# A layer of two linear-recurrence mixers: the block products of the triangular inverses run over four 32x32 tiles in slots of eight systems, and the planner's tables are set anew

## The chip, the cores and the metric

The kernel runs on one core of a Trainium2 chip. The metric is the device time of one execution in microseconds (us). The kernel before took 1860.27 us as the median of 3 runs (1856.26 to 1860.48).

## The reference, cut to what matters

One layer of a diffusion backbone works on 1024 latent tokens and 128 context tokens of width 1024, in fp32. A combined projection feeds two token mixers, an output projection follows, and then a gated MLP with a depthwise convolution. The first mixer (HGRN2) has 4 heads of 128. The second (RWKV-7) has 8 heads of 64 and this recurrence, run forwards and backwards:

```python
def step(S, inp):
    r_t, w_t, k_t, v_t, kk_t, a_t = inp
    sk = jnp.einsum('bhij,bhj->bhi', S, kk_t)
    S = (S * w_t[:, :, None, :] - sk[..., None] * (kk_t * a_t)[:, :, None, :]
         + v_t[..., None] * k_t[:, :, None, :])
    return S, jnp.einsum('bhij,bhj->bhi', S, r_t)
```

Each state update depends on the one before it through `sk`. The kernel works in chunks of 64 tokens: inside a chunk the dependence is a unit triangular 64x64 system, one for each chunk, head and direction, and the kernel forms the inverse of every one of them ahead of the recurrence.

## The kernel before, in words

**Stages.** The numbers are those of the profiled execution. From 0 to about 50 us the inputs are loaded, normalised and turned. From 50 to 500 us the combined projection runs: dense products of the normalised tokens `hh`, `hl` with weights `wh`, `wl`, each product in three parts (L1108, L1109, L1110), 128x128 weights against 384 columns. Among them lie the features of the RWKV mixer for four pairs of heads (`features`, L1346 to L1475) and, after each pair, `elim`, which makes the inverses. From 495 us the two chains of the recurrence run (`prep`, first line on TensorE L1759, then `chains`, L1803 to L1831), 18 chunk steps for each of two groups, with the HGRN blocks (L1629 to L1674), the rest of the projection and the loads of the modulation weights (`ada_block`, L1009 to L1023) among them. The output projection (L1995 to L1997) follows from about 950 us, the MLP's first half (L2104) from 1088 us and its down projection (L2253 to L2255) from 1570 us.

**The inverses.** A 64x64 triangular system is cut into 32x32 quarters. VectorE inverts the two diagonal quarters of all systems at once, one row after another (L1488, L1491, 31 steps), and turns the result with two transposes into `ttd` and `tn` (L1493, L1494). The off-diagonal quarter of the inverse is a product of three 32x32 matrices: first the middle product of `ako` with `tn` (L1507), then that result with `ttd` (L1516). Systems lie in pairs: `c2` is 0 or 1, and pair member `c2` has its upper half on partitions `64*c2` to `64*c2+31` and its lower half on the next 32. So both products of a system go from one group of 32 partitions to its neighbour. `elim` is called five times: for four pairs of heads with 32 pairs of systems each (`nu` = 32), and for the context chunks with 16.

In the kernel before, the products go in halves of 16 pairs of systems. For each half a batch of 32 products runs L1507 (two tiles of the array, one for each `c2`, each with a PSUM bank of its own), two evictions copy 32 partitions x 512 elements to `pm` (L1510), a batch of 32 products runs L1516, and two evictions copy to the result `tt` (L1519). An fp32 product counts as two MATMUL instructions in the trace, so a batch has 64. There are 9 batches of each kind. The corner of `tt` that must be zero is written by GpSimd ahead of all this (L1500), and the result goes to DRAM in 24 transfers for each call (L1530 to L1545), some of them of those zeros. The chains load it again, step by step.

**What sets the order.** Nothing is issued where it is written. A planner (`Plan`) records every operation, and a list scheduler puts each engine's operations in an order by their longest path to the end plus a lead in us: `LEADS` has one for each function, `NUDGE` one for each stretch of 64 operations. PSUM tiles come from named sets of places; the `el` set of `elim` lies on banks 6 and 7, which the chains' set `a` uses as well, and a tile of `a` isn't placed before all earlier tiles of `el` are. So the chains' first product stands behind the last batch of the context's `elim`. The order that results is fixed when the kernel is built; each engine then runs its list in order. Transfers are issued by SP or by GpSimd, whichever the planner picks.

The diff touches `elim`, `pbank`, the `el` set, `ada_block` and the two tables.

Of the kernel before, what the change touches and what calls it, by code (L numbers as in the profile page):

```python
# [34 lines left out]
EARLY = ()  # L35
LEAD_EARLY = -1.6
# [9 lines left out]
NUDGE = {1: -6, 3: 10, 38: 17, 47: 42, 56: -15, 59: 1, 63: 5, 79: -4, 90: -3, 93: 10, 94: 10, 95: -10, 96: -10, 97: 10, 98: 30, 99: 10, 100: 20, 101: -10, 108: -10, 109: -10, 110: -6, 111: -10, 114: -3, 122: -2, 129: 11, 130: 10, 131: 10, 132: 10, 134: -44, 136: 10, 138: 40, 141: -8}  # L46
LEADS = {'hgrn_block': -3.6, 'hgrn_out': 106.6, 'ada_block': 46.6, 'prep': 119.5, 'mod_scale': 90, 'const': 103.8, 'params': -71.6, 'param_loads': -28.9, 'wo_tile': 8.1, 'ffn_down': 14.5, 'chains': 18.7, 'hgrn_in': 0.0, 'features': 0.0, 'elim': -12.5, 'post': 12.6, 'conv_rkv': 0.0, 'bonus_rows': 5.2, 'turned': 2.4, 'step_kernel': -1.0}
# [753 lines left out]
def step_kernel(ctx: ExitStack, tc: tile.TileContext, I, O):  # L801
# [73 lines left out]
    at = {t: plan.tags[t].places[0][1] for t in ("tsys", "etmp", "ttd", "tn")}  # L875
    plan.tag("adaw3", [(top, at[t] + 512 * b) for t in ("ttd", "tn", "tsys") for b in range(2)], 512)
    plan.tag("adab3", [(top, at["etmp"])], 128)
    plan.tag("adam3", [(top, at["etmp"] + 128)], 128)
# [59 lines left out]
    banks("el", 6, 2)  # L938
# [9 lines left out]
    def pbank(tag="pj"):  # L948
        return tl(tag, [P, 512])
# [51 lines left out]
    def ada_block(b):  # L1001

        c0, early = 2048 + 512 * b, b in EARLY
        br = tl("adab3" if early else "adab", [4, P])
        ld(br, I["ada_b"][0, c0:c0 + 512].rearrange("(a b) -> a b", b=P))
        ps, mr = pbank("el" if early else "a"), tl("adam3" if early else "adam", [P, P])
# [3 lines left out]
        for kt in range(KT):  # L1010
            w = tl("adaw3" if early else "adaw2", [P, 512])
            ld(w, I["ada_w"][0, kt * P:(kt + 1) * P, c0:c0 + 512])
            with plan.together():
                for q in range(4):
                    mm(ps[32 * q:32 * q + 32, 0:P], sT[:, kt, :], w[:, P * q:P * q + P], False, kt == KT - 1)
# [6 lines left out]
        pq = pbank("el" if early else "a")  # L1022
# [455 lines left out]
    def elim(akd, ako, nu, name, tag):  # L1478
# [18 lines left out]
        pm = tl("asys", [P, 32, 32])  # L1497
        copy(tt[:, :, 0:32], ttd[:, :, 0:nu].rearrange("p t u -> p u t"))
        for c2 in range(2):
            pool.memset(tt[64 * c2 + 32:64 * c2 + 64, :, 32:64], 0.0)  # L1500
        for u0 in range(0, nu, 16):
            ps = [pbank(tag) for c2 in range(2)]
            with plan.together():
                for u in range(u0, u0 + 16):
                    for c2 in range(2):
                        a, b = slice(64 * c2, 64 * c2 + 32), slice(64 * c2 + 32, 64 * c2 + 64)
                        mm(ps[c2][b, (u - u0) * 32:(u - u0) * 32 + 32], ako[a, u, :], tn[a, :, u], True, True)  # L1507
            for c2 in range(2):
                b = slice(64 * c2 + 32, 64 * c2 + 64)
                copy(flat(pm[b, u0:u0 + 16, :]), ps[c2][b, :])  # L1510
            ps = [pbank(tag) for c2 in range(2)]
            with plan.together():
                for u in range(u0, u0 + 16):
                    for c2 in range(2):
                        a, b = slice(64 * c2, 64 * c2 + 32), slice(64 * c2 + 32, 64 * c2 + 64)
                        mm(ps[c2][a, (u - u0) * 32:(u - u0) * 32 + 32], pm[b, u, :], ttd[b, :, u], True, True)  # L1516
            for c2 in range(2):
                a = slice(64 * c2, 64 * c2 + 32)
                copy(tt[a, u0:u0 + 16, 32:64], ps[c2][a, :].rearrange("p (u t) -> p u t", t=32))  # L1519
# [829 lines left out]
```

## Time and profile before

| | us |
|---|---|
| median of 3 runs | 1860.27 |
| profiled execution, its own time | 1852.33 |
| its span | 1850.2 |
| TensorE busy | 1785.8 |
| VectorE busy | 1417.0 |
| ScalarE busy | 868.0 |
| GpSimd busy | 296.2 |

The profiled execution lies 7.9 us under the median of the runs. TensorE's busy time is a union of overlapping matmuls. A row of a timeline gives the start, the duration and the count of merged instructions; the time between the starts of two neighbouring rows is what the first of them costs the engine. A row of a grouped view gives the total busy time and the mean duration of one, then the idle time of the engine ahead of the group and what ended it. "issue" is time in which the engine waited for nothing that the profile shows.

### The profile page before, as it was taken

How to read it: one execution, taken by the hardware profiler on the slowest of the kernel's cores; microseconds unless marked ns; L12 is line 12 of the kernel's file. 1: busy time of each engine (PE TensorE's matmuls, PEld its weight loads, DVE VectorE, ACT ScalarE, POOL GpSimd, SP SyncE). 2: the span in 40 equal slices, each digit the busy share in tenths (PEclk: the TensorE clock that was granted, in tenths of full speed). 3: DMA queues.
4: the chain of work that ended last, by engine and by line, in shares of the span. 5: the costliest groups of instructions: out<-in, count | busy, mean ns of one | idle time of the engine just before them, and what ended most of it. 6: DMA issues, size and time to landing. Idle time of an engine off the chain costs nothing.

```text
span 1850.2 us, 45135 instructions
## 1 busy us (share of the span) xinstructions
PE 1785.8 (97%) x18369; PEld 1598.8 (86%) x18369; DVE 1417.0 (77%) x2660; ACT 868.0 (47%) x1755; POOL 296.2 (16%) x567
## 2 busy tenths in 40 slices
PE   7999999899989999999999989999999999999998
PEld 4889898799977888888778789999999999888886
DVE  7559888977778887885787688999999954896443
ACT  7556755642256544553545754444444433422321
POOL 2113425253212212212210100000000000000000
PEclk9999999999999999999999999999999999999999
DMA  9325637476667757889977611222222245775351
GB/s 324 105 74 141 153 92 189 114 206 185 198 189 223 233 177 219 268 239 288 288 247 252 211 49 59 96 72 72 72 72 72 80 144 207 244 251 191 120 172 59
DMA packets 268728, 307.44 MB, mean 166 GB/s; under 512 B 63292, under 2 KB 212842, under 8 KB 268521
## 3 DMA queue, kind: packets, MB, share of 16 engines
q1 hardware_dynamic: 241112, 220.92, 40.1%
q0 software_dynamic: 27408, 83.64, 13.3%
q8 instruction: 144, 2.36, 0.5%
q14 instruction: 64, 0.52, 0.1%
HBM read 200.50 MB, written 103.99 MB: 165 GB/s over the span
## 4 chain that ended last, share of the span: by engine, by line
PE 81%; DVE 7%; DMA 6%; issue 3%; ACT 2%; POOL 1%; SPq 0%; DVEq 0%; POOLq 0%; ACTq 0%
PE banks L2104 26%; PE banks L1108 6%; PE banks L1110 5%; PE banks L1109 5%; PE banks L2253 5%; PE banks L2254 5%; PE banks L2255 5%; PE banks L1995 2%; PE banks L1759 2%; PE banks L1996 1%; PE banks L1997 1%; DMA top<-in_ada_w_dram 1%; PE banks L1803 1%; PE banks L1810 1%; PE banks L1674 1%
## 5 line engine op out<-in xcount | busy, mean ns | idle before, releaser
L1108 PE MATMUL banks<-hh,wh 128*128 128x384 f32 x768 | 280.7, 365 | 0.0
L1110 PE MATMUL banks<-hh,wl 128*128 128x384 f32 x768 | 259.6, 338 | 0.1
L1109 PE MATMUL banks<-hl,wh 128*128 128x384 f32 x768 | 259.4, 338 | 0.0
L2193 DVE SCALAR_TENSOR_TENSOR low<-low,pf 128x1024 f32<-128x1024 f32 x176 | 224.4, 1278 | 3.5 <-ACT low L2187 2.1
L2104 PE MATMUL banks<-qm,wh 128*128 128x320 f32 x968 | 224.5, 311 | 0.0
L2104 PE MATMUL banks<-qm,wl 128*128 128x320 f32 x528 | 163.8, 310 | 3.3 <-DVE wl L2074 3.3
L2104 PE MATMUL banks<-hbm,wh 128*128 128x256 f32 x880 | 162.8, 282 | 2.4 <-DVE low L1975 1.6
L1108 PEld LDWEIGHTS banks<-hh,wh 128*128 128x128 f32 x768 | 145.9, 190 | 20.4 <-issue 12.3
L2104 PEld LDWEIGHTS banks<-qm,wh 128*128 128x128 f32 x968 | 161.9, 190 | 0.1
L1109 PEld LDWEIGHTS banks<-hl,wh 128*128 128x128 f32 x768 | 146.2, 190 | 2.0 <-issue 1.0
L1110 PEld LDWEIGHTS banks<-hh,wl 128*128 128x128 f32 x768 | 145.6, 190 | 0.0
L2104 PEld LDWEIGHTS banks<-hbm,wh 128*128 128x128 f32 x880 | 139.2, 190 | 2.8 <-ACT hbm L2037 1.8
L2104 PE MATMUL banks<-ham,wh 128*128 128x256 f32 (+1 forms) x616 | 132.4, 295 | 0.0
L2104 PE MATMUL banks<-hbm,wl 128*128 128x256 f32 x440 | 124.4, 283 | 0.0
L2104 PEld LDWEIGHTS banks<-qm,wl 128*128 128x128 f32 x528 | 99.6, 189 | 3.9 <-DVE wl L2074 3.9
L2104 PEld LDWEIGHTS banks<-ham,wh 128*128 128x128 f32 x616 | 102.4, 191 | 0.0
L2142 ACT COPY fx<-banks 128x320 f32<-128x320 f32 (+1 forms) x132 | 52.2, 396 | 84.0 <-PE banks L2104 83.8
L2074 ACT CAST wh<-fx 128x512 fp32r<-128x512 f32 x88 | 54.3, 620 | 75.1 <-PE banks L2104 65.3
L2253 PE MATMUL banks<-qm,hbm 128*128 128x512 f32 x216 | 85.6, 396 | 0.0
L2254 PE MATMUL banks<-qm,hbm 128*128 128x512 f32 x216 | 85.5, 396 | 0.0
L2255 PE MATMUL banks<-qm,hbm 128*128 128x512 f32 x216 | 85.4, 395 | 0.0
L2104 PEld LDWEIGHTS banks<-hbm,wl 128*128 128x128 f32 x440 | 83.8, 191 | 0.0
(508 smaller groups left out, 4364.4 us busy)
## 6 DMA issues: line engine op xcount, KB each, us to landing
wr<-in_w_in_dram SPq DMA_DIRECT2D x34, 512.0 KB, 6.0
top<-in_ada_w_dram SPq DMA_DIRECT2D x64, 256.0 KB, 5.5
d_a<-low POOLq DMA_DIRECT2D x22, 576.0 KB, 4.0
low<-d_ak SPq DMA_DIRECT2D x64, 192.0 KB, 4.9
low<-in_ffn_w_up_dram SPq DMA_DIRECT2D x22, 512.0 KB, 3.9
wr<-in_ffn_w_gate_dram SPq DMA_DIRECT2D x22, 512.0 KB
low<-d_kb SPq DMA_DIRECT2D x36, 256.0 KB, 3.6
low<-d_a SPq DMA_DIRECT2D x12, 704.0 KB, 4.8
```

What stands on the lines that cost most here:

```text
L1108: mm(o, wh[:, kt, :], hh[:, kt, c], kt == 0, False)
L1109: mm(o, wh[:, kt, :], hl[:, kt, c], False, False)
L1110: mm(o, wl[:, kt, :], hh[:, kt, c], False, kt == KT - 1)
L1759: mm(pa[h][:, P * w:P * w + P], kb[hc[h], w, :], W[hc[h], A0[h] + 192 * w:A0[h] + 192 * w + P], True, True)
L1995: mm(ps, oh[:, kt, :], woh, kt == 0, False)
L2074: split(*w, src)
L2104: pe.matmul(o, a[:, kt, :], b[:, kt, :], start=start and first, stop=last, skip_group_check=not start)
L2142: act.copy(keep[n], y[:, 0:w])
L2193: dve.scalar_tensor_tensor(av, shifted(dy, dx), tap(3 * dy + dx), av, MUL, ADD)
L2253: mm(o, lh, w[:, 0, c], first, False)
L2254: mm(o, lh, w[:, 1, c], False, False)
L2255: mm(o, ll, w[:, 0, c], False, last)
```

## The change

The two products of the inverses are interleaved. The systems go in groups of eight pairs, one group for each slot. Slot `k` holds the first product of group `k` (from the even groups of 32 partitions to the odd ones) and the second product of group `k-1` (from the odd to the even ones). All four groups of partitions are in use, and the four tiles take turns, product by product. All four write one PSUM tile of 256 columns, half a bank. One eviction of 128 partitions x 256 elements then moves both results to `tt`: the finished quarter to its place, and the middle product into the corner of `tt` that the next slot reads as weights. The first slot holds only first products, the last only second ones; their evictions take 32 partitions x 256 twice. A call with 32 pairs has five slots, the one with 16 has three. Since the zero corner now serves as a buffer, GpSimd writes its zeros after the last slot.

The tables that set the order are changed in a few entries, for example the lead of `elim` from -12.5 to -4.6. Code for an early block of modulation weights, which an empty list had switched off, is removed.

```diff
-NUDGE = {..., 98: 30, 99: 10, 100: 20, ..., 129: 11, 130: 10, ...}
-LEADS = {..., 'param_loads': -28.9, 'wo_tile': 8.1, ..., 'elim': -12.5, ..., 'bonus_rows': 5.2, ...}
+NUDGE = {..., 98: 47, 99: 5, 100: 20, ..., 126: 17, 127: 24, 130: 10, ...}
+LEADS = {..., 'param_loads': 9.6, 'wo_tile': 5.1, ..., 'elim': -4.6, ..., 'bonus_rows': 6.6, ...}
...
-    banks("el", 6, 2)
+    plan.tag("el", [(mp, 512 * 6 + 256 * b) for b in range(4)], 256)
...
-    def pbank(tag="pj"):
-        return tl(tag, [P, 512])
+    def pbank(tag="pj", n=512):
+        return tl(tag, [P, n])
...
-        pm = tl("asys", [P, 32, 32])
+        pm = tl("asys", [P, 8, 32])
         copy(tt[:, :, 0:32], ttd[:, :, 0:nu].rearrange("p t u -> p u t"))
-        for c2 in range(2):
-            pool.memset(tt[64 * c2 + 32:64 * c2 + 64, :, 32:64], 0.0)
-        for u0 in range(0, nu, 16):
-            ps = [pbank(tag) for c2 in range(2)]
-            with plan.together():
-                for u in range(u0, u0 + 16):
-                    for c2 in range(2):
-                        a, b = slice(64 * c2, 64 * c2 + 32), slice(64 * c2 + 32, 64 * c2 + 64)
-                        mm(ps[c2][b, (u - u0) * 32:(u - u0) * 32 + 32], ako[a, u, :], tn[a, :, u], True, True)
-            for c2 in range(2):
-                b = slice(64 * c2 + 32, 64 * c2 + 64)
-                copy(flat(pm[b, u0:u0 + 16, :]), ps[c2][b, :])
-            ps = [pbank(tag) for c2 in range(2)]
-            with plan.together():
-                for u in range(u0, u0 + 16):
-                    for c2 in range(2):
-                        a, b = slice(64 * c2, 64 * c2 + 32), slice(64 * c2 + 32, 64 * c2 + 64)
-                        mm(ps[c2][a, (u - u0) * 32:(u - u0) * 32 + 32], pm[b, u, :], ttd[b, :, u], True, True)
-            for c2 in range(2):
-                a = slice(64 * c2, 64 * c2 + 32)
-                copy(tt[a, u0:u0 + 16, 32:64], ps[c2][a, :].rearrange("p (u t) -> p u t", t=32))
+        q = [slice(32 * i, 32 * i + 32) for i in range(4)]
+        last = nu // 8
+        for k in range(last + 1):
+            ps = pbank(tag, 256)
+            low_ = (lambda u: pm[:, u]) if k == 1 else (lambda u, k=k: tt[:, 8 * (k - 2) + u, 32:64])
+            with plan.together():
+                for u in range(8):
+                    o = slice(32 * u, 32 * u + 32)
+                    for i in range(4):
+                        if i % 2 == 0 and k < last:
+                            mm(ps[q[i + 1], o], ako[q[i], 8 * k + u, :], tn[q[i], :, 8 * k + u], True, True)
+                        if i % 2 and k:
+                            mm(ps[q[i - 1], o], low_(u)[q[i]], ttd[q[i], :, 8 * (k - 1) + u], True, True)
+            pv = ps.rearrange("p (u t) -> p u t", t=32)
+            if k and k < last:
+                copy(tt[:, 8 * (k - 1):8 * k, 32:64], pv)
+            else:
+                for i in (0, 2):
+                    if k:
+                        copy(tt[q[i], 8 * (k - 1):8 * k, 32:64], pv[q[i]])
+                    else:
+                        copy(pm[q[i + 1]], pv[q[i + 1]])
+        for i in (1, 3):
+            pool.memset(tt[q[i], :, 32:64], 0.0)
```

In the kernel after the change the first product is L1503 and the second L1505; the evictions are L1514 (first slot), L1508 (middle slots) and L1512 (last slot), the zeros L1516; lines outside `elim` stand six lower (L1108 is L1102, L1759 is L1753).

**TensorE, the fourth pair's inverses.** One product to a row, or a count of equal rows behind it. Before:

```order
L1507 MATMUL banks<-top 32x32 x32
L1108 MATMUL banks<-hh,wh_132 128x384
L1109 MATMUL banks<-hl,wh_132 128x384
L1110 MATMUL banks<-hh,wl_134 128x384
L1516 MATMUL banks<-top 32x32 x32
```

After the change, the first slot and the start of the second:

```order
L1503 MATMUL banks<-top 32x32 x16
L1102 MATMUL banks<-hh,wh_132 128x384
L1103 MATMUL banks<-hl,wh_132 128x384
L1104 MATMUL banks<-hh,wl_134 128x384
L1102 MATMUL banks<-hh,wh_132 128x384
L1103 MATMUL banks<-hl,wh_132 128x384
L1104 MATMUL banks<-hh,wl_134 128x384
L1503 MATMUL banks<-top 32x32
L1505 MATMUL banks<-top 32x32
```

Batches of 32 products with one line each have become slots of 16, then 32 with the two lines in turn; between slots stand six products of the projection here, where three stood between two batches.

**TensorE, from the context's inverses to the chains.** Before, the last batch and what follows it:

```order
L1110 MATMUL banks<-hh,wl_134 128x384
L1516 MATMUL banks<-top 32x32 x32
L1759 MATMUL banks<-low 128x128 x16
L1285 MATMUL banks<-c_ident,fx 128x128 x3
L1773 MATMUL banks<-c_ident,low 128x128 x4
```

After the change, the last of three slots and what follows it:

```order
L1104 MATMUL banks<-hh,wl_134 128x384
L1505 MATMUL banks<-top,fx 32x32 x16
L1753 MATMUL banks<-low 128x128 x16
L1279 MATMUL banks<-c_ident,fx 128x128 x3
L1102 MATMUL banks<-hh,wh_131 128x384
```

The chains' first product still stands right behind the last products of the inverses. Counted over the two orders, 1848 products of the projection stand ahead of it before and 1872 now: there are 24 between the two batches before, and 24 between each two of the three slots now.

**GpSimd, the zeros of the context's result** (`d_akp` is its place in DRAM). Before:

```order
L1500 MEMSET fx 32x16x32
L1543 DMA d_akp_79<-fx 32x4x32
L1543 DMA d_akp_81<-fx 32x4x32 x2
L1295 DMA d_hf_97<-fx 128x384
L1500 MEMSET fx 32x16x32
```

After the change:

```order
L1542 DMA d_akp_79<-fx 32x4x64 x2
L1516 MEMSET fx 32x16x32
L1540 DMA d_akp_79<-fx 32x4x32
L1542 DMA d_akp_81<-fx 32x4x64 x2
L1540 DMA d_akp_81<-fx 32x4x32
L1516 MEMSET fx 32x16x32
```

The zeros and their transfers now stand among the transfers of the finished quarters instead of ahead of them.

More of the change, by code (lines that the diff above doesn't have):

```diff
@@ L34 @@
 STRETCH = 2.76
-EARLY = ()
-LEAD_EARLY = -1.6
 LEAD_LAST = 300.0
@@ L45 @@
 BUSY = 186.0
-NUDGE = {1: -6, 3: 10, 38: 17, 47: 42, 56: -15, 59: 1, 63: 5, 79: -4, 90: -3, 93: 10, 94: 10, 95: -10, 96: -10, 97: 10, 98: 30, 99: 10, 100: 20, 101: -10, 108: -10, 109: -10, 110: -6, 111: -10, 114: -3, 122: -2, 129: 11, 130: 10, 131: 10, 132: 10, 134: -44, 136: 10, 138: 40, 141: -8}
-LEADS = {'hgrn_block': -3.6, 'hgrn_out': 106.6, 'ada_block': 46.6, 'prep': 119.5, 'mod_scale': 90, 'const': 103.8, 'params': -71.6, 'param_loads': -28.9, 'wo_tile': 8.1, 'ffn_down': 14.5, 'chains': 18.7, 'hgrn_in': 0.0, 'features': 0.0, 'elim': -12.5, 'post': 12.6, 'conv_rkv': 0.0, 'bonus_rows': 5.2, 'turned': 2.4, 'step_kernel': -1.0}
+NUDGE = {1: -6, 3: 10, 38: 17, 47: 42, 56: -15, 59: 1, 63: 5, 79: -4, 90: -3, 93: 10, 94: 10, 95: -10, 96: -10, 97: 10, 98: 47, 99: 5, 100: 20, 101: -10, 108: -10, 109: -10, 110: -6, 111: -10, 114: -3, 122: -2, 126: 17, 127: 24, 130: 10, 131: 10, 132: 10, 134: -44, 136: 10, 138: 40, 141: -8}
+LEADS = {'hgrn_block': -3.6, 'hgrn_out': 106.6, 'ada_block': 46.6, 'prep': 119.5, 'mod_scale': 90, 'const': 103.8, 'params': -71.6, 'param_loads': 9.6, 'wo_tile': 5.1, 'ffn_down': 14.5, 'chains': 18.7, 'hgrn_in': 0.0, 'features': 0.0, 'elim': -4.6, 'post': 12.6, 'conv_rkv': 0.0, 'bonus_rows': 6.6, 'turned': 2.4, 'step_kernel': -1.0}
 C_W0, C_A0, C_KK, C_KA, C_RK, C_LNW, C_LNB = 0, 8, 12, 16, 20, 24, 28
@@ L874, in step_kernel @@
         .add("tn", 1024)
[L875 to L878, printed above, removed]
     Layout(fx, 0, NX).add("tt", 2048).add("wlora", 512).add("ha", 384, 2).add("hb", 384, 2)
@@ L1001, in ada_block @@
     def ada_block(b):
-        c0, early = 2048 + 512 * b, b in EARLY
-        br = tl("adab3" if early else "adab", [4, P])
+        c0 = 2048 + 512 * b
+        br = tl("adab", [4, P])
         ld(br, I["ada_b"][0, c0:c0 + 512].rearrange("(a b) -> a b", b=P))
-        ps, mr = pbank("el" if early else "a"), tl("adam3" if early else "adam", [P, P])
+        ps, mr = pbank("a"), tl("adam", [P, P])
         with plan.together(mr):
@@ L1010, in ada_block @@
         for kt in range(KT):
-            w = tl("adaw3" if early else "adaw2", [P, 512])
+            w = tl("adaw2", [P, 512])
             ld(w, I["ada_w"][0, kt * P:(kt + 1) * P, c0:c0 + 512])
@@ L1021, in ada_block @@
                 st(g2d[:, 512 * (b - 6) + P * q:512 * (b - 6) + P * q + P], mr[32 * q:32 * q + 2, :])
-        pq = pbank("el" if early else "a")
+        pq = pbank("a")
         pe.transpose(pq[:, 0:P], mr, ident)
@@ L1560, in conv_rkv @@
         return t
-    with plan.ahead(LEAD_EARLY):
-        for b in EARLY:
-            ada_block(b)
     kv = [conv_rkv(0, 1), conv_rkv(0, 2)]
@@ L1919, in post @@
         split(oh[:, 4:8], ol[:, 4:8], ps.rearrange("p (k t) -> p k t", k=4))
-    late = [b for b in range(8) if b not in EARLY]
     cg = [chains(0), chains(1)]
@@ L1927, in step_kernel @@
         if n % 2 == 0 and n:
-            if n // 2 - 1 in late:
+            if n // 2 <= 8:
                 with plan.ahead(LEAD_LAST if n // 2 > 6 else LEAD_ADA):
```

## The prediction

> **What bounds the kernel now.** I read the page first, then the busy time by stage, then the chain of waits around the place that changes. From the page:
>
> ```profile
> span 1850.2 us, 45135 instructions
> PE 1785.8 (97%) x18369; PEld 1598.8 (86%) x18369; DVE 1417.0 (77%) x2660; ACT 868.0 (47%) x1755; POOL 296.2 (16%) x567
> PE 81%; DVE 7%; DMA 6%; issue 3%; ACT 2%; POOL 1%; SPq 0%; DVEq 0%; POOLq 0%; ACTq 0%
> ```
>
> TensorE (PE) is busy for 97% of the span, and 81% of the chain that ended last is TensorE's own work. So a microsecond of TensorE's time counts, unless the stage in which it is saved waits for something else. The stages:
>
> ```profile
> core 0: us, PE busy (x) PEld busy (x) DVE busy (x) ACT busy (x) POOL busy (x), PEclk, DMA share, GB/s
> 196.00:300.00 104.00, 103.31 (x1286) 90.60 (x1285) 90.71 (x179) 69.16 (x135) 43.70 (x80) 0.98 0.58 147
> 300.00:400.00 100.00, 94.62 (x1207) 83.87 (x1206) 79.89 (x165) 54.91 (x115) 46.47 (x83) 0.95 0.57 146
> 400.00:500.00 100.00, 99.29 (x897) 96.29 (x896) 81.68 (x176) 28.24 (x46) 33.63 (x61) 0.97 0.67 196
> 500.00:600.00 100.00, 90.23 (x2069) 76.79 (x2070) 76.33 (x185) 56.72 (x139) 18.50 (x37) 0.97 0.71 208
> 600.00:700.00 100.00, 96.01 (x1768) 83.76 (x1767) 82.57 (x200) 50.34 (x121) 19.66 (x39) 1.00 0.69 209
> 700.00:800.00 100.00, 94.13 (x1860) 80.97 (x1860) 77.27 (x192) 50.18 (x110) 20.82 (x43) 1.00 0.80 243
> ```
>
> The inverses lie between 196 and 495 us. There TensorE idles 0.7, 5.4 and 0.7 us in the three rows, so this stage is TensorE's. In the chains' stage it idles 9.8, 4.0 and 5.9 us: still mostly TensorE's, but with waits. VectorE (DVE) is busy for 80 to 87% and is the next in line. At the border the chain of waits runs through the products themselves:
>
> ```profile
> 486.78 0.18 PE banks L1110
> 486.96 1.92 PE banks L1507 x64
> 488.88 0.48 PE banks L1285 x3
> ...
> 493.37 0.18 PE banks L1110
> 493.55 1.92 PE banks L1516 x64
> 495.47 1.99 PE banks L1759 x32
> ```
>
> Each batch costs 1.92 us, and the chains (L1759) start the moment the context's last batch ends.
>
> **The products.** A batch of 64 instructions uses two tiles, 32 for each, so a tile takes 1.92 / 32 = 0.06 us for one. All batches are alike:
>
> ```profile
> L1516 PE MATMUL banks<-top 32*32 32x32 f32 x576 | 18.3, 228 | 0.0
> L1507 PE MATMUL banks<-top 32*32 32x32 f32 x576 | 18.2, 228 | 0.5 <-ACT fx L1519 0.3
> ```
>
> 576 of each line are 9 batches, 18 in all: 18 x 1.92 = 34.6 us are removed. (The 36.5 us of these two rows hold the modelled ends as well.) In their place come four calls of five slots and one of three: 23 slots, 13 middle ones with 64 instructions on four tiles and 10 outer ones with 32 on two. In either kind a tile has 16 instructions. What four tiles in turn do is shown by another line, whose 24 instructions go over four tiles, 6 for each:
>
> ```profile
> 512.42 0.40 PE L1629 MATMUL banks<-top 128*32 128x32 f32 x24
> 512.75 0.28 PE L1803 MATMUL banks<-low 128*64 128x64 f32 x2
> ```
>
> They cost 0.33 us, 0.055 for each instruction of a tile, about what a tile takes in a batch of two, though twice as many tiles work. So four tiles run beside one another. By this row a slot costs 16 x 0.055 = 0.88 us; half a batch (0.96) with a fixed end of 0.16 on top is 1.12. I take 1.0, between the two: 23.0 us, with 20.2 and 25.8 as ends. The products change by 23.0 - 34.6 = -11.6 us (-14.4 to -8.8).
>
> [...]
>
> **The visits.** TensorE pays to leave the projection's products and to come back:
>
> ```profile
> 280.72 0.44 PE L1108 MATMUL banks<-hh,wh 128*128 128x384 f32 x1
> 281.01 0.34 PE L1109 MATMUL banks<-hl,wh 128*128 128x384 f32 x1
> 281.18 0.34 PE L1110 MATMUL banks<-hh,wl 128*128 128x384 f32 x1
> 281.45 1.99 PE L1507 MATMUL banks<-top 32*32 32x32 f32 x64
> 283.37 0.44 PE L1108 MATMUL banks<-hh,wh 128*128 128x384 f32 x1
> 283.65 0.34 PE L1109 MATMUL banks<-hl,wh 128*128 128x384 f32 x1
> 283.82 0.34 PE L1110 MATMUL banks<-hh,wl 128*128 128x384 f32 x1
> ```
>
> Products follow one another every 0.17 us, but the start of the batch comes 0.27 after the last of them, and the second product 0.28 after the first behind the batch: 0.10 + 0.11 = 0.21 us for a visit. Counted over the two orders, there are 435 changes between the dense products (projection, output, MLP) and everything else before, and 465 now: 15 visits more, 7 of them ahead of the chains and most of the others in the chains' stage. They cost 15 x 0.21 = 3.1 us; 1.1 if only the five additional slots pay.
>
> **The evictions.** Before:
>
> ```profile
> L1519 ACT COPY fx<-banks 32x512 f32<-32x512 f32 x15 | 8.6, 575 | 11.9 <-PE banks L1516 11.7
> L1510 ACT COPY top<-banks 32x512 f32<-32x512 f32 x12 | 7.0, 580 | 11.5 <-PE banks L1507 11.3
> L1510 DVE COPY top<-banks 32x512 f32<-32x512 f32 x6 | 4.2, 693 | 5.7 <-PE banks L1507 5.6
> L1519 DVE COPY fx<-banks 32x512 f32<-32x512 f32 x3 | 2.0, 676 | 2.1 <-PE banks L1516 2.1
> ```
>
> That is 36 evictions, 21.8 us. Now there are 33 of 256 columns, 24 on ScalarE and 9 on VectorE in the new order. The nearest rows:
>
> ```profile
> L1855 ACT COPY top<-banks 64x256 f32<-64x256 f32 x59 | 21.6, 366 | 18.8 <-PE banks L1831 11.9 <-DVE top L1855 6.2
> L1805 DVE COPY low<-banks 128x256 f32<-128x256 f32 x11 | 4.5, 421 | 4.0 <-PE banks L1810 2.1 <-PE banks L1803 1.8
> ```
>
> 24 x 0.37 + 9 x 0.42 = 12.7 us, so 9 us leave ScalarE and VectorE. TensorE's own work hides them already, so I count nothing; if VectorE were the bound, its 2.4 us (6.2 - 3.8) would be the gain.
>
> What the evictions add is a wait. Slot after slot needs the one before it: 18 such places, where 9 second batches waited for a first. Behind a waiting slot stands all of TensorE's list. The tightest place before:
>
> ```profile
> 428.98 1.99 PE banks L1507 x64
> 431.69 2.23 PE banks L1516 x64
> ```
>
> The order has three projection products there, and the second batch starts 431.69 - 428.98 - 1.92 = 0.8 us after the first has ended. So 0.8 us is about what an eviction needs from end to start. Now at least six products (1.0 us) stand between two slots at the places I looked at, up to 24 (4.1 us). I count 0.6 us in all, twice the 0.3 us that ScalarE's eviction L1519 cost in the row of L1507 above; 0 at least, and the dear end is a rival below.
>
> **The zeros.** GpSimd's writes cost
>
> ```profile
> L1500 POOL MEMSET fx<- 32x1024 f32 (+1 forms) x10 | 8.7, 874 | 0.5
> ```
>
> the same ten as before, now behind the last slot, with the transfers of the lower quarters behind them on GpSimd and SP. What waits for them is the chains' loads. For the last pair some 290 projection products (50 us) lie between its last slot and the chains. The context's result is needed at the eleventh chunk step, whose `prep` (the first group's) stands at
>
> ```profile
> 777.38 1.16 PE L1759 MATMUL banks<-low 64*128 64x128 f32 x16
> ```
>
> some 280 us later. So nothing is counted; without that cover, two writes of 0.9 us and their transfers would be late.
>
> **The order.** Up to the first slot TensorE's order is the same, so nothing ahead of 196 us moves. The start of the chains: the four pairs' products go from 16 x 1.92 = 30.7 to 20.0 us (-10.7). The context's go from two batches with 24 products between them (3.84 + 4.1 = 7.9) to three slots with 48 (3.0 + 8.2 = 11.2, +3.3). Seven visits add 1.5. So the chains start 5.9 us earlier, at 489.5, and 24 projection products (4.1 us) that stood behind that point are done already. From the thirteenth chunk step on TensorE's order is nearly the old one, and as many products lie ahead of it. Between 196 and 800 us the idle time is 26.4 us, and a new order deals it out anew. If all six rows were as good as the best (0.7), 22 us would go; if all were as bad as the worst (9.8), 32 would come. Both orders hold the same work, so I take 0, with 4.5 either way (half the spread of two rows).
>
> **The sum.** -11.6 + 3.1 + 0.6 = -7.9 us against the profiled execution's 1852.33: 1844.4. The median of the runs is 7.9 us above that execution, and I carry this over: 1860.27 - 7.9 = 1852.4, so 1852.
>
> **The rivals.**
>
> *The chains' stage doesn't take the gain.* If the recurrence's own steps set the pace from 495 us on, only its earlier start counts; the 24 products done early leave TensorE idle later. For it speak the 9.8 us of idle time in 500 to 600; against it the 94 to 96% of the next rows. Time: -5.9 and 1.5 for the later visits, -4.4: 1855.9.
>
> *Four tiles are no faster than two.* If starts in this tiling stay as far apart as in a batch (1.92 / 64 = 30 ns), a middle slot takes 1.92: 13 x 1.92 + 10 x 1.0 = 35.0, +0.4, with 3.7 for visits and evictions +4.1: 1864.4. The pace of L1629 speaks against it, but its tiles have 128 rows, and no line before drives four groups of 32 rows. [...]
>
> *The row groups take turns at the bank.* Before, the two tiles of a batch write two banks; now four groups of rows write one. If they go one by one, each instruction costs a tile's 0.06: 13 x 64 x 0.06 + 10 x 32 x 0.06 = 69.1 us, +34.5 and 3.7: 1898. [...] L1629's four tiles do share a bank, but they are column tiles.
>
> *The evictions come late (the other side).* Place: the 18 points between slots. An evicting engine may be in the middle of something longer:
>
> ```profile
> L1276 ACT CAST wh<-wr 128x1024 fp32r<-128x1024 f32 x20 | 21.0, 1048 | 23.8 <-PE banks L1109 19.7 <-DVE top L1491 3.4 <-DMA top<-in_ada_w_dram 0.5
> ```
>
> With 1.05 us ahead of it an eviction takes 1.85 of which six products cover 1.0: 0.8 x 18 = 14 us, in place of the 0.6, +5.5: 1865.8. It decides from a mean wait of 8.5 / 18 = 0.5 us. The wider places of the order speak against it.
>
> **How the numbers follow.** Forecast 0.58; the chains' stage 0.24; late evictions 0.08; no faster than two 0.06; turns at the bank 0.04. The forecast's own range is 1847 to 1857, from the ends of the slot's cost and the idle time. The range 1844 to 1865 leaves out the bank, most of the late evictions and the forecast's low end, about 0.15. About 0.3% (5.6 us, 1854.7) can be told from no change: faster 0.58 (0.53 of the forecast, 0.05 of the second case), same 0.31 (0.05, 0.19, 0.06 and 0.01), slower 0.11.
>
> **What would show it.** Right: a middle slot of 64 instructions costs about 1.0 us; TensorE's busy time falls by some 11 us; L1753 starts near 489.5; hardly any idle time ahead of L1503 and L1505. Wrong: a middle slot near 1.9 or 3.8 (pace, bank); idle time ahead of slots put down to L1508 or L1514 (late evictions); the chains early, but more idle time between 490 and 800 (the chains' stage, or the new order).

## The result and the profile after

The changed kernel takes **1832.33 us** (median; 1824.9 to 1835.64) where the kernel before beside it takes 1858.63: a ratio of 0.9872 (95% interval 0.9844 to 0.99). Three more sets of its runs gave 0.9861, 0.9858 and 0.9862, each within 0.0025. So it is faster by some 25 us, three times the 7.9 us that were forecast, and below the range.

The profiled execution of the changed kernel took 1824.9 us. Its page, with the rows that answer to those of before (span, busy time, the chain by engine):

```profile
span 1823.1 us, 45165 instructions
PE 1767.2 (97%) x18369; PEld 1578.1 (87%) x18369; DVE 1413.7 (78%) x2667; ACT 858.9 (47%) x1744; POOL 302.3 (17%) x570
PE 84%; DMA 5%; DVE 5%; issue 3%; ACT 2%; SPq 1%; POOL 0%; DVEq 0%; POOLq 0%; ACTq 0%
```

The span is 27.1 us shorter, TensorE's busy time only 18.6 (1785.8 to 1767.2); the other 8.5 us are idle time of TensorE. VectorE does as much as before (1413.7 us against 1417.0). The stages (stretch, its length, busy time of PE, PEld, DVE, ACT and POOL, then the granted clock, the DMA engines' share and GB/s):

```profile
196.00:300.00 104.00, 103.49 (x1439) 89.86 (x1438) 93.84 (x182) 72.44 (x151) 50.76 (x93) 1.00 0.63 156
300.00:400.00 100.00, 96.28 (x1131) 86.12 (x1131) 88.17 (x190) 53.09 (x112) 45.28 (x80) 0.98 0.67 175
400.00:500.00 100.00, 97.74 (x1055) 90.67 (x1050) 73.83 (x158) 25.14 (x46) 34.65 (x61) 1.00 0.68 193
500.00:600.00 100.00, 95.65 (x2200) 82.24 (x2200) 86.53 (x221) 60.25 (x148) 22.89 (x45) 1.00 0.76 225
```

Two things stand out against the four rows of before. In 500 to 600 us TensorE is busy for 95.65 us in place of 90.23. And the clock column reads 1.00, 0.98, 1.00, 1.00 where it read 0.98, 0.95, 0.97, 0.97: a column that the prediction quoted and did not use.

**The slot costs what was forecast.** The chain of waits of the changed kernel at its first slot and at the start of the chains (start, duration, what):

```profile
196.59 1.01 PE banks L1503 x32
...
481.11 1.01 PE banks L1505 x32
482.11 1.98 PE banks L1753 x26
```

That is the outer kind. A middle slot, 64 instructions on four tiles, in the timeline (start, duration, engine, line):

```profile
200.61 0.34 PE L1104 MATMUL banks<-hh,wl 128*128 128x384 f32 x1
200.88 0.22 PE L1503 MATMUL banks<-top 32*32 32x32 f32 x1
...
201.74 0.23 PE L1505 MATMUL banks<-top 32*32 32x32 f32 x1
201.90 0.83 PE L1384 MATMUL banks<-hsum,top 128*128 128x2 f32 x6
```

From 200.88 to 201.90 are 1.02 us: four tiles run beside one another for the price of two (1.01), and their starts are 16 ns apart (1.02 / 64). Nor do the evictions come late: the groups of both lines have no idle time ahead of them.

```profile
L1503 PE MATMUL banks<-top 32*32 32x32 f32 x576 | 19.5, 228 | 0.0
L1505 PE MATMUL banks<-top,fx 32*32 32x32 f32 x416 | 14.1, 227 | 0.0
```

(The two lines take turns, so their modelled times overlap; 23 slots of 1.01 are 23.2 us.)

**What was not in the sum.** In the trace of before the granted clock is 1.00 nearly everywhere and 0.50 in a few spells. One of them, in rows of 1 us:

```profile
353.00:354.00 1.00, 1.00 (x8) 1.00 (x8) 1.00 (x3) 0.17 (x1) 0.32 (x1) 0.67 0.00 0
354.00:355.00 1.00, 1.00 (x8) 1.00 (x6) 0.27 (x2) 0.77 (x2) 0.38 (x1) 0.50 0.23 45
355.00:356.00 1.00, 1.00 (x5) 1.00 (x4) 0.59 (x2) 0.19 (x1) 0.61 (x2) 0.50 0.76 129
356.00:357.00 1.00, 1.00 (x5) 1.00 (x5) 0.93 (x5) 0.00 (x0) 0.48 (x1) 0.63 0.44 104
357.00:358.00 1.00, 1.00 (x8) 1.00 (x7) 0.97 (x2) 0.00 (x0) 0.80 (x2) 1.00 1.05 331
```

The spell lasts 3.4 us, in which 1.7 us of TensorE's work are lost, while its busy time reads 1.00. Summed over the spells up to TensorE's last product ((1 - clock) x time), 17.1 us are lost before and 5.1 after; 1.6 us of before's sum fall on time in which TensorE idles, so 15.5 and 5.1 count. So the 27.1 us are about 10.4 of clock, 8.5 of idle time, and 8.2 of work at full clock (18.6 - 10.4; forecast for products and visits: 8.5).

One pair of traces says little on clock and idle time, since both scatter between executions (before's clock loss by 3.7 us, as a standard deviation over its runs; the changed kernel's waits from 26.9 to 28.8 us in four traces). But every run lists its mean granted clock. So each run's time splits into clock lost, (1 - clock) x time, and a rest. This loss is an upper bound of the time that the clock costs: it also counts 1.5 to 2.9 us of half clock behind TensorE's last product, in every kernel, and half clock while TensorE waits. The means over all runs that list a clock (the last column is explained with the experiments):

| kernel | runs | mean us | clock lost us | rest us | low windows |
|---|---|---|---|---|---|
| before | 58 | 1855.8 | 22.0 | 1833.9 | 7.0 |
| changed | 17 | 1830.3 | 11.1 | 1819.2 | 0.7 to 1.6 |
| e1 slots, old tables | 4 | 1838.2 | 13.8 | 1824.4 | 2.7 |
| e2 batches, new tables | 4 | 1880.3 | 31.0 | 1849.2 | 5.7 |
| e3 two tiles at a time | 4 | 1837.6 | 11.5 | 1826.1 | 2.7 |
| e4 batches doubled | 6 | 1867.1 | 25.2 | 1841.9 | 9.3 |
| e5 batches apart | 12 | 1858.2 | 23.2 | 1835.0 | 5.9 |
| e6 slots close | 8 | 1847.0 | 21.2 | 1825.7 | 5.1 |
| e7 new LEADS only | 4 | 1835.2 | 14.7 | 1820.5 | 2.6 |
| e8 new NUDGE only | 4 | 1837.1 | 12.4 | 1824.7 | 2.3 |
| e9 sums later | 6 | 1835.0 | 14.1 | 1820.9 | |
| e10 waits filled, dense | 4 | 1828.7 | 5.0 | 1823.7 | |
| e12 waits filled, small | 5 | 1835.3 | 11.0 | 1824.3 | |
| e11 before, waits filled | 12 | 1852.0 | 20.2 | 1831.7 | 4.7 |
| e13 MLP's waits filled | 5 | 1830.4 | 8.1 | 1822.4 | |

The change of 25.5 us is 10.9 of clock and 14.6 of the rest. The standard errors of a rest and of a loss are 0.3 to 0.5 us for before and 0.4 to 2.7 in the sets of four. One run of e12 took 9500.21 us, at a clock of 1.0, and is left out here and below.

### The profile page after: what moved, and what is told of

Read it like the earlier page. It is cut to its first block, busy times and chain, and to the rows that moved or that the text cites. A ratio compares the mean times of both kernels' runs of the same rounds, so it can differ in the third digit from the quotient of the medians.

```text
span 1823.1 us, 45165 instructions
## 1 busy us (share of the span) xinstructions
PE 1767.2 (97%) x18369; PEld 1578.1 (87%) x18369; DVE 1413.7 (78%) x2667; ACT 858.9 (47%) x1744; POOL 302.3 (17%) x570
## 4 chain that ended last, share of the span: by engine, by line
PE 84%; DMA 5%; DVE 5%; issue 3%; ACT 2%; SPq 1%; POOL 0%; DVEq 0%; POOLq 0%; ACTq 0%
PE banks L2097 27%; PE banks L1102 7%; PE banks L1104 6%; PE banks L1103 6%; PE banks L2246 5%; PE banks L2247 5%; PE banks L2248 5%; PE banks L1988 2%; PE banks L1990 2%; PE banks L1989 2%; PE banks L1753 2%; DMA low<-d_ak 1%; PE banks L1797 1%; PE banks L1340 1%; DMA top<-in_ada_w_dram 1%
## 5 line engine op out<-in xcount | busy, mean ns | idle before, releaser
L1102 PE MATMUL banks<-hh,wh 128*128 128x384 f32 x768 | 280.4, 365 | 0.2 <-DVE fx L1291 0.2
L2186 DVE SCALAR_TENSOR_TENSOR low<-low,pf 128x1024 f32<-128x1024 f32 x176 | 224.8, 1279 | 14.1 <-ACT low L2180 12.4
L1102 PEld LDWEIGHTS banks<-hh,wh 128*128 128x128 f32 x768 | 144.6, 188 | 18.8 <-issue 10.0
L2135 ACT COPY fx<-banks 128x256 f32<-128x256 f32 (+1 forms) x132 | 52.2, 396 | 87.2 <-PE banks L2097 86.8
L2246 PE MATMUL banks<-qm,hbm 128*128 128x512 f32 x216 | 85.6, 396 | 0.0
```

The costliest lines, as they stand in the source:

```text
L1102: mm(o, wh[:, kt, :], hh[:, kt, c], kt == 0, False)
L2135: act.copy(keep[n], y[:, 0:w])
L2186: dve.scalar_tensor_tensor(av, shifted(dy, dx), tap(3 * dy + dx), av, MUL, ADD)
L2246: mm(o, lh, w[:, 0, c], first, False)
```

## The experiments

**Slots and tables apart.** The change has two parts: the slots, and new numbers in NUDGE and LEADS. e1 takes the slots with the old tables, e2 the batches with the new ones.

```
e1:  changed kernel, NUDGE and LEADS of before
e2:  kernel before, NUDGE and LEADS of the change
```

> The slots of the changed kernel with the two tables of the kernel before. Theory (three parts: the products' own time -8 us with visits; spells of half granted clock, which cost 17 us of clock before and 6 after; idle time in the chains' stage, which the new tables deal out anew, -8 us): the first two parts come with the slots, the third with the tables, so 1840 us, mean granted clock 0.993 or more, idle TensorE time between 480 and 800 us as before. Rival (the tables do it, the slots give only their products' time): 1850 us. Rival (the slots do all of it): 1832 us.

> The batches of the kernel before with the two tables of the changed kernel. Theory: only the idle time goes, the spells of half clock stay (granted clock 0.989 to 0.990): 1850 us. Rival (the tables do it): 1838 to 1842 us. Rival (the tables were fitted to the slots, and alone do nothing or harm): 1858 us or more.

Measured: e1 1838.0 us, ratio 0.9915 (0.9891 to 0.9938); e2 1880.25, 1.0144 (1.0121 to 1.0166). The slots alone bring 17.6 us: 9.5 of the rest, 8.2 of clock. The tables bring the other 7.9: 5.2 of the rest, 2.7 of clock. The split of the clock is rough: the standard error of e1's loss alone is 2.7 us, and against the 11 runs of before in its own set (mean 1854.1) e1 is 15.9 us faster, not 17.6. With the batches the same tables cost 24.5 us, so they are worth nothing by themselves; they were fitted to the slots.

Which table it is was asked with two more kernels, e7 (the changed kernel with the old NUDGE) and e8 (with the old LEADS).

> The changed kernel with the old table NUDGE and the new LEADS. If the new tables' gain over the slots alone (1838.0 to 1830.6) lies in the lead of the inverses (-12.5 to -4.6), which moves the slots among the projection products: the chains start near 483 us as in the changed kernel, 1832 us. If it lies in NUDGE, whose changed entries stand for late operations: the chains start near 483 too, but 1838 us.

> The changed kernel with the old LEADS and the new NUDGE. If the tables' gain lies in LEADS: the chains start near 490 us as with both old tables, 1838 us. If in NUDGE: 1832 us.

Measured: e7 1834.03, 0.9891 (0.9864 to 0.9917); e8 1836.92, 0.9901 (0.9877 to 0.9925). The intervals cover each other; the chains start at 490.9 and 484.9 us, the other way round than expected. This stays open: neither mean (1835.2 and 1837.1) can be told from e1's 1838.2, and four runs don't part them.

**Is it the four tiles, or the order?** e3 keeps the changed kernel's order, and lets a middle slot do all products of one line and then all of the other.

```diff
                 e, l = op.forms[0]
+                if e == "PE" and op.kind == "elim":
+                    l = sorted(l, key=lambda i: i[3])
                 for v in op.tiles:
```

> The changed kernel, every engine's order kept, but inside each middle slot first the 16 products of the one kind and then the 16 of the other, so that two tiles are at work at a time. Theory: a middle slot costs 1.9 us in place of 1.0, 13 x 0.9 = 12 us, and some spells of half clock come back (3 to 8 us): 1847 to 1852 us. Rival (the clock has nothing to do with the products' tiles): 12 us only, 1844 us, granted clock as in the changed kernel. Rival (the extra TensorE time is hidden by idle time): under 1838 us.

Measured: 1837.87 us, 0.9911 (0.9893 to 0.993); beside the changed kernel's 1830.3 its rest is 6.9 us longer and its clock loss the same (11.5 against 11.1). In its trace a middle slot takes 1.70 us (202.61 to 204.31), since the second half starts while the first ends (the two lines mix from 203.29 to 203.46): 13 x 0.69 = 9.0 us were to be paid. So the tiles side by side are worth 7 us, all of it work, and the clock gain does not come from them.

**Does the clock follow how much of the array works?** e4 repeats each product of a batch into the other 32 output partitions, so that four tiles work in before's order.

```diff
+                if e == "PE" and op.kind == "elim":
+                    l = self.doubled(l)   # each pair of products, then the same pair into the neighbouring 32 partitions
...
```

> The kernel before, every engine's order kept, but each product of a batch is done a second time into the neighbouring 32 partitions of its bank, which nobody reads: four tiles at work in place of two, twice the instructions. The batch should still cost about 1.9 us if the four run beside one another. Theory (the granted clock follows how much of the array works over a few us): the spells behind the two close pairs of batches (295 to 299 and 431 to 439 us) go or get shorter, granted clock 0.992, 1853 us. Rival (a spell comes from the time without wide products, whatever the small ones do): spells as before, 1858 us. Rival (the doubled batch costs more, 2.5 us or over): 1868 us or more.

Measured: 1866.92 us, 1.007 (1.0053 to 1.0088). A batch takes 2.13 us, and the clock loss is 25.2 us: not less than before's 22.0. The theory's forecast fell, but the theory was hardly tested: a doubled batch still uses four tiles of 32x32, a quarter of the 128x128 that a product of the projection has in the trace. And the doubled batches brought waits of their own. Between 196 and 490 us the trace has 5.6 us in which TensorE waits for nothing that the profile shows, 4.8 of them ahead of the batches' products, where before has none; with 18 x 0.21 = 3.8 us for the batches this covers the 8.0 us that the rest grew.

**Do the spells stand behind close batches?** Two spells of before follow places where two batches have only three products between them. e5 puts twelve more there.

```diff
-        self.schedule()
+        self.schedule(); self.later([(1434, 4), (2223, 4), (2220, 4), (2217, 4)])   # move an operation and what follows from it behind so many triples
...
+Plan.later = later
```

> The kernel before in its own frozen order, but for four batches (and what follows from them) that move behind twelve more products of the projection each, so that the two places where two batches stand with only three products between them have 15 there. Clock theory: the half-clock spells at 295 to 299 and 431 to 439 us in the trace of before (1.7 and 3.6 us of clock lost) stand behind just those two places and vanish; no other change; 5 us less than before, 1850 us beside 1855. Rival (the spells fall where they do by chance of the execution, or come from the summing products behind the batch at 294.5, not from the batches): the spells stay within a few us of their places, and the time is that of before within 1.5 us.

Measured: 1858.95 us, 1.0007 (0.9989 to 1.0025); clock loss 23.2. The theory in this form fell too, and the trace shows why. The same rows around the first batch, before:

```profile
195.49 0.91 PE L1346 MATMUL banks<-low,fx 32*128 32x384 f32 x2
196.33 1.99 PE L1507 MATMUL banks<-top 32*32 32x32 f32 x64
198.25 0.45 PE L1108 MATMUL banks<-hh,wh 128*128 128x384 f32 x1
...
199.60 0.33 PE L1109 MATMUL banks<-hl,wh 128*128 128x384 f32 x1
```

and in e5, whose order is the same up to here:

```profile
197.37 0.91 PE L1346 MATMUL banks<-low,fx 32*128 32x384 f32 x2
198.21 1.99 PE L1507 MATMUL banks<-top 32*32 32x32 f32 x64
200.13 0.45 PE L1108 MATMUL banks<-hh,wh 128*128 128x384 f32 x1
...
201.51 0.53 PE L1108 MATMUL banks<-hh,wh 128*128 128x384 f32 x1
```

Behind the same batch the products take 0.53 us in the one execution and 0.33 in the other. So a spell is decided by something that differs from run to run. In the traces it is where a grid lies. In windows of 0.1 us the spells of before last 3.4 or 6.8 us and start at

```
295.3  353.3  367.0  431.8  544.5  1066.7  1080.4 us     remainders by 3.4133 us:  1.76 1.73 1.78 1.72 1.79 1.75 1.80
```

The divisor is measured too: from the start at 295.3 to the one at 1066.7 us are 771.4 us, 226 times 3.4133. In e5 the nine starts leave remainders of 3.02 to 3.10, in the changed kernel the three ahead of TensorE's last product 2.00 to 2.06. In all 18 traces of the runs here, starts and ends lie on a grid of 3.41 us within 0.1, with another offset in each execution. Laid on the rows of TensorE between 196 and 486 us, the grid's windows at full clock divide by the share that the projection's products fill:

| dense share of the window | windows | followed by half clock |
|---|---|---|
| under 0.25 | 50 | 34 |
| 0.25 to 0.4 | 80 | 10 |
| over 0.4 | 1335 | 0 |

Most of the windows under 0.25 hold idle time: counted again with slightly other borders they are 48, TensorE idles for more than 5% of 31 of them, and 29 of these are followed by half clock; of the 17 that idle less only 3 are. One of the three, in e2:

```profile
283.90 0.34 PE L1110 MATMUL banks<-hh,wl 128*128 128x384 f32 x1
284.17 0.92 PE L1411 MATMUL banks<-low,fx 32*128 32x384 f32 x4
...
285.65 2.00 PE L1507 MATMUL banks<-top 32*32 32x32 f32 x64
287.58 0.69 PE L1108 MATMUL banks<-hh,wh 128*128 128x384 f32 x1
```

Half clock starts at 287.5 us, behind 3.4 us of small products without a gap. So here half clock came behind small products alone; behind the other 14 of the 17 it did not.

Nor does the bound of 0.25 hold outside this stage. Between 486 and 950 us, 795 windows at full clock have under a quarter of products of 128x128 with 384 or more columns, and TensorE idles for at most 5% of them: none is followed by half clock. What sorts the windows of all stages better is a sum over all products. Give each product the share that its weights have of 128x128, the largest form in the trace, times its columns of data, and divide a window's sum by that of the fullest. Under 0.15, 46 of 47 windows at full clock are followed by half clock; from 0.15 to 0.3, 49 of 243; from 0.3 to 0.4, 4 of 679; above, none of 8191. This count was made on the traces afterwards, and no run tested it.

So a stretch of 3 to 6 us that is poor in dense products covers a whole window of 3.41 us, or doesn't, by where the execution's grid lies. Its price is a likelihood: for every offset of the grid I counted the windows under 0.25 between 194 us and the chains, and the mean over the offsets is the last column of the table. Before has 7.0, the changed kernel 0.7 to 1.6; 5.8 windows fewer at 1.7 us are 9.9 us if every one is followed by half clock (34 of 50 were), and 10.9 were measured over the whole run. The column does not order every kernel: e5 has 1.1 windows fewer than before and lost 1.2 us more, and of the 28.5 us that e2's trace lost, 21.7 lie behind 500 us.

**The converse.** e6 brings the slots of the changed kernel close together.

```diff
+        self.schedule(); self.later([(982, 4), (980, 7), (977, 12), (1431, 3), (1429, 8), (1426, 12), (1880, 3), (1878, 6), (1875, 9)])
```

> The changed kernel in its own frozen order, but in the first three calls the first four slots stand with only three products between them, in place of 12 to 18; the products that stood there come ahead of them. Clock theory: four slots of 1.0 us and three gaps of 0.8 make a stretch of 6.4 us that is one quarter dense products (the close batches before: 4.6 us, one ninth dense), so spells of 3.4 to 6.8 us come back behind them, three times 1.7 to 3.4 us lost, and 0.2 us of waiting for an eviction at nine places: 7 to 12 us slower than the changed kernel, 1840 to 1845 us. Rival (the clock does not depend on how close the slots stand): only the waits, 2 us slower, 1834 us, no spell behind the three calls.

Measured: 1845.9 us, 0.995 (0.993 to 0.9969): by the means 16.7 slower than the changed kernel, 10.1 of it clock, as forecast (5 to 10), and 6.5 the rest (forecast 2). But more than the slots' distance had changed. With the products moved ahead, TensorE waits for 16.6 us between 196 and 490 us, against 5.7 in the changed kernel; the two largest sums, as the line that waited, what for, the sum, how often and the longest:

```profile
PE banks L1384 <- DVE top L1380: 6.6, 2, 5.1
PE banks L1503 <- issue: 3.4, 2, 2.6
```

The spells of its trace in that stretch start at 203, 217, 353 and 370 us, beside waits of 1.5, 2.6, 2.4 and 5.1 us that end at 201, 218, 354 and 373. So the loss came back, but e6 does not show that the closeness of the slots alone brings it. e9 tried the other way, to put products ahead of the summing products that wait at 345 us.

```diff
+        self.schedule(); self.later([(2022, 9)])
```

> The changed kernel in its own frozen order, but the summing products of one pair's last third (L1384 at 345.04 us, before which TensorE idles 2.36 us for VectorE's L1485, with a half-clock spell of 4 us behind it) and what follows from them stand behind nine more triples of projection products. Clock theory: the products cover the idle time and the spell does not come: 2.3 and 2.0 us less, 4 us faster than the changed kernel, 1828 us where that has 1832. Rival (the wait only moves: VectorE is what this stage then waits for, some products later): within 1.5 us of the changed kernel.

Measured: 1834.24 us, 0.9885 (0.9864 to 0.9907), with the changed kernel at 1830.74 beside it; clock loss 14.1 against 10.5. That is 3.5 us slower, more than either expected. As the rival had it, the wait moved: TensorE now waits 1.89 us ahead of L1279, for ScalarE's L1275. The spell behind it stayed (345.7 us), and two others came, at 359 and 366 us.

**The clock by itself.** e10 to e12 change no order and add products. Where TensorE waits for another engine, the last dense product is repeated into the bank that the waiting operation overwrites (e10, e11), or small products of the same length (e12).

```diff
-                e, l = op.forms[0]
+                e, l = op.forms[0]; self.cover(op)   # repeats the last dense product COVER[op.id] times ahead of op
...
+COVER = {2022: 12, 5876: 11, 5976: 12}               # L1384 at 345 us; L2097's first; L2097's first on ham
...
```

> The changed kernel with three of TensorE's waits filled: ahead of L1384 at 345.04 us (2.36 us of waiting), of the MLP's first product at 1034.88 (3.01) and of its first one on ham at 1052.19 (2.03), the last dense product is repeated 12, 11 and 12 times into the bank that the waiting operation overwrites; nothing else changes. Window theory (the granted clock halves for 3.41 us behind each stretch of a fixed 3.41-us grid in which dense products fill less than about a quarter): the repeats cost nothing, being in waits, and the spells at 346, 1040 and 1053 us go: 1.5 and 3.4 us less, 5 us faster than the changed kernel, 1826 us beside 1831; clock 0.997. Rival (the spells belong to waits on other engines, whatever TensorE does meanwhile): the same as the changed kernel or up to 2 us slower, since the repeats may run over.

> As the run with three waits filled, but with small products: 35, 42 and 29 fp32 products of 32x32 on two tiles in turn, as long in all as the dense ones there. Window theory (only dense products hold the clock): the spells at 346, 1040 and 1053 stay, and the time is the changed kernel's 1831 within 1.5 us. Rival (any work of TensorE holds the clock): 5 us faster, as the run with dense products.

> The kernel before with four of its waits filled in the same way by repeated dense products: ahead of L1390 at 352.57 (2.76 us) and at 368.49 us (1.80), and of the MLP's first products at 1065.31 (2.95) and 1078.60 (1.56). Window theory: the spells at 353, one and a half of the two at 367, and those at 1067 and 1080 us go: 1.7 + 2.6 + 3.4 = 8 us less, 1848 us beside 1856; the spells behind batches at 295 and 432 stay where the grid of the execution has them. Rival: as before within 2 us.

Measured: e10 1828.57 us, 0.9851 (0.9829 to 0.9873); e12 1835.45, 0.9886 (0.9863 to 0.9909); the changed kernel beside them 1830.12. The MLP's start in the three traces, in one row of 30 us each, e10 first:

```profile
1040.00:1070.00 30.00, 25.69 (x167) 23.07 (x166) 28.04 (x53) 20.91 (x43) 2.25 (x3) 1.00 0.24 82
```

then e12:

```profile
1040.00:1070.00 30.00, 25.74 (x264) 23.39 (x263) 28.00 (x50) 20.63 (x41) 2.17 (x3) 0.83 0.22 75
```

and the changed kernel beside them:

```profile
1036.00:1066.00 30.00, 21.98 (x135) 20.00 (x135) 27.76 (x52) 20.50 (x42) 2.05 (x3) 0.89 0.23 79
```

With dense products in the waits the clock is 1.00; with small products it is 0.83, which can't be told from that with the waits left idle (0.89): one piece of 3.41 us makes 0.06 in such a row. Between the runs of e10 and e12 stand 6.6 us, and 6.0 of clock loss (5.0 against 11.0). So in e10 dense work in the waits held the clock at 1.00 over these 30 us. That small work doesn't is not shown as cleanly, since the small repeats were shorter than planned and left more of each wait. What remains of the MLP's first wait (the bracket at the end: us of idle time, and what ended it), in e10:

```profile
1045.72 0.42 PE L2097 MATMUL banks<-qm,wl 128*128 128x320 f32 x1 [0.52 <-DVE wl L2067]
```

and in e12:

```profile
1047.80 0.41 PE L2097 MATMUL banks<-qm,wl 128*128 128x320 f32 x1 [1.37 <-DVE wl L2067]
```

At the other two places 0.20 and 0.27 us remain in e10, 1.03 and 0.97 in e12. The repeats were not free, either: against the changed kernel both lost about 5 us of the rest, and e10's net gain is 1.5 us, inside the intervals. In e10's trace the spells at 346, 1040 and 1053 us are gone, as expected, but one of 6.8 us came at 365. In e12's the two of the MLP came (at 1048 and 1062), but the one at 346 did not, against the theory. e11 gave 1851.86 us, 0.9978 (0.9958 to 0.9998), half of the 8 us expected, and only 1.8 us less of clock loss (20.2 against 22.0): the spells at 353 and 1067 were gone, one stayed at 1077, and others fell at 520 and 602.

To keep the gain without the fill at 345 us, e13 filled the two waits of the MLP alone.

> The changed kernel with only the two waits of the MLP's start filled by dense repeats (11 ahead of its first product, 12 ahead of its first one on ham); the wait at 345 us is left as it is. Window theory: from the MLP's first product to L2246 the changed kernel took 505.0, 505.3 and 505.3 us in three traces, the one with three waits filled 501.7; this keeps that gain of 3.5 us without what the fill at 345 us cost: 1827 us beside 1830.5, clock 0.996. Rival (each edit of the order gives back elsewhere what it wins): 1830 us or more.

Measured: 1829.34 us, 0.9865 (0.984 to 0.9889), beside 1829.84 for the changed kernel: no faster, so the rival held. The 3.5 us were mostly never there to keep. In the changed kernel the 3.01 us of waiting stand behind the MLP's first products; in e10 and e13 the repeats stand ahead of those, so a stretch that starts with them (501.7 us in e13, 506.1 in the changed kernel beside it) leaves the filled wait out. From the start of the last product of the output projection to L2246 the changed kernel takes 505.2, 505.6, 505.5 and 506.3 us in its four traces, and e10 and e13 504.4: a gain of 1.3. Over its runs e13 lost 8.1 us of clock where the changed kernel lost 11.1, but its rest is 3.1 longer; part of that can be clock that was lost while TensorE waited anyway, and the remainder is open. So no version here beats the changed kernel by what can be measured.

The changed kernel itself ran three more times beside others, with this expectation and two like it:

> The changed kernel itself beside the others on this chip. Every theory: 1832 us where before has 1858, a ratio of 0.986 to 0.988; its profile has 5 to 9 us of lost clock, and spells at 346 and 1040 us if these belong to the order and not to the one execution.

It gave 1830.74, 1830.12 and 1829.84 us. A spell that starts at 345 to 347 us and one that starts at 1053 to 1057 are in all four of its traces; those at 1040, 561, 887 and 924 to 930 in one or two.

## Why the prediction was wrong

- **The products: right.** "I take 1.0, between the two: 23.0 us": a slot costs 1.01 to 1.02 in either kind. The fixed end of 0.16 us in its upper bound was the author's estimate; 0.05 of it shows (1.01 against 16 x 0.06). Both rivals on its pace fell: the starts are 16 ns apart, not 30, and four row groups write one bank in 1.02 us, where turns of 0.06 us for each of 64 instructions would take 3.84.
- **The visits and the evictions: right in sign, small.** No slot waited for an eviction; the rest of e1, -9.5 us, lies 1.6 from the forecast's -7.9, which had slots, visits and evictions and nothing else. Part of this nearness is chance: e1's trace also has 3.9 us fewer waits between 196 and 1035 us than before's (30.8 against 34.7), which the forecast put at nothing.
- **The order: the step that failed first.** "Both orders hold the same work, so I take 0, with 4.5 either way." With the new tables the rest falls by 5.2 us more (e1 against the changed kernel). It is mostly idle time: TensorE's waits between 196 and 1035 us are 34.7 us before, 30.8 in e1's trace, and 26.9, 27.1, 27.0 and 28.8 in the four traces of the changed kernel. Most of it goes from waits for nothing that the profile shows (11.5 us before, 1.8 to 4.3 in the changed kernel). The waits of 500 to 700 us, as the line that waited, what for, the sum, how often and the longest, before:

```profile
PE banks L1818 <- issue: 5.5, 3, 3.7
PE banks L1629 <- DVE top L1655: 2.3, 3, 1.3
```

and in the changed kernel:

```profile
PE banks L1825 <- issue: 1.2, 1, 1.2
PE banks L1753 <- DMA low<-d_ak: 0.9, 2, 0.6
```

The wait of 3.7 us begins at 542 us, while the queue of data transfers alone takes 92% of the DMA engines' time (541 to 546 us) and one block of instructions (one packet, 0.02 MB) comes over a queue of its own. That the block was late is the author's guess, which no run tried; and it was not tried why the new order has fewer such waits.
- **The granted clock: the term that was missing, and the larger step that failed.** The rows that the prediction quoted read 0.95 to 0.98 over the inverses, some 10 us of lost work in 300, and the sum treated them as given. The change halves the loss of the whole run (22.0 to 11.1 us). This was the larger half of the miss, 10.9 of 17.6 us (25.5 - 7.9), as far as lost clock is lost time. The likely reason: 1.0 us of small products with 2 to 3 us of dense ones behind it leaves few windows empty of dense work (0.7 to 1.6 by the table), where 1.92 us, with L1346, L1411 or a wait beside it, left more (7.0). The slots with the old tables (e1, 13.8 us) and slots with two tiles at a time (e3, 11.5) fit this; how much of it is the small products and how much the waits beside them, no run separates.
- **The chains** started at 482.0 (482.0 to 485.9 in four traces) in place of 489.5: of the 7.5 us more, 8.5 are the clock loss of 196 to 500 us, 10.2 before and 1.7 after. The rival "the chains' stage doesn't take the gain" was wrong in its direction: that stage gave 7 us of idle time back (13.8 to 6.6 between 500 and 700; 5.9 to 8.7 in the other three traces).
- **The margin.** The prediction carried 7.9 us over from the profiled execution to the median of three runs. Over 58 runs before's mean is 1855.8, 3.5 above that execution: by it the forecast would have been 1848, still 18 too high.

## What to carry to other kernels

Look at the granted clock in the rows by stage before counting microseconds: here it read 0.95 to 0.98 over the inverses, and of the 47 windows of 3.41 us at full clock whose sum over the products was under 0.15, 46 were followed by half clock, which cost up to 1.7 us for a piece of 3.41 us on top of the stretch's own time. With the same tables, slots of 1.0 us among dense products lost 13.8 us of clock where batches of 1.92 us lost 22.0, about as much as the rest won (8.2 and 9.5 us in e1). When an edit moves work, look at the waits that it makes before putting its clock down to the work. A table of numbers that sets the order is fitted to one set of pieces, and with another it can cost more than the change brings.

## What the hardware showed that was not expected

- The half clock came in pieces of 3.41 us on a grid, with another offset in each of the 18 traces; in before's it runs from the spell at 295 us to the one at 1080 (remainders 1.72 to 1.80); the clock lost per run scatters by 3.7 us before (standard deviation; the time goes from 1849 to 1865 us) and by 2.0 in the changed kernel. That this scatter is where the grid falls is inferred.
- Doubling the tiles at work in a batch did not help the clock (25.2 us lost against 22.0), and small products in the MLP's waits did not (0.83 against 0.89 with the waits idle), though they left up to 1.4 us of a wait idle; useless dense products did (1.00).
- Four tiles of 32x32 that write four quarters of one half bank ran side by side: 64 instructions in 1.02 us, 32 on two tiles in 1.01.
